# Dilated attention trunk on one core: softmax maxima and sums exchanged by a mask and two short matmuls, merge and turning inside pairs

## The chip, the cores and the metric

One core of a Trainium2 chip, one launch. The time is the device time of that core in microseconds (us). TensorE (PE) multiplies, VectorE (DVE) and ScalarE (ACT) work on elements, GpSimd (POOL) does a little of both and issues adding DMAs, SyncE (SP) issues the other DMAs. Each engine runs its own instructions in order; semaphores tie them together.

## The reference

A trunk of two layers over 512 tokens of width 1024, in float32. Layer 0 mixes tokens by three groups of dilated sliding-window attention, layer 1 by causal pooling; each is followed by a SwiGLU FFN (2816 wide), and a last RMSNorm. The part that matters here is the attention: eight heads of 128, each in three groups.

```python
ATTN_PAIRS = ((128, 1), (512, 4), (2048, 16))     # window, dilation
def dilated_attention_mixer(h, w_qkv, w_out):
    qkv = (h @ w_qkv).reshape(B, S, N_ATTN_GROUPS, 3, HEADS_PER_GROUP, HEAD_DIM)
    for g, (window, dil) in enumerate(ATTN_PAIRS):
        o, lse = dilated_window_attention(qkv[:, :, g, 0], qkv[:, :, g, 1], qkv[:, :, g, 2], window, dil, slopes[g])
        outs.append(o)
        lses.append(lse)
    o = jnp.stack(outs, axis=0)
    wts = jax.nn.softmax(jnp.stack(lses, axis=0), axis=0)
    o = jnp.sum(wts[..., None] * o, axis=0).reshape(B, S, ATTN_WIDTH)
    return o.astype(h.dtype) @ w_out
```

The three groups' outputs of a head are weighted by their softmax denominators. So a token needs one common maximum and one common sum over the scores of all three groups.

## The kernel before

**Products.** All large products are taken in a 32-bit form that TensorE multiplies in one pass (fp32r), with each operand split into a high and a low part: hi·hi, hi·lo and lo·hi. Weights come by SP DMAs into `raw` buffers; ScalarE rounds them to `whi` (L79), VectorE subtracts to `wlo` (L80). A product of queries and keys of one head and group is done by `seven` (L383): seven half-size products in place of eight, each of 4 x 3 matmuls of 128x256 (L374 to L376), 84 in all. Between the seven products stand `behind(0)` to `behind(6)`; there `pump()` prepares the next weights, and pieces of other work can be hung in through `after`. The weights of a `seven` are sums of blocks: one DMA of GpSimd adds on loading (L139), and VectorE adds twice more (L152, L153), on the same in-order queue that evacuates the products (L414 to L424). `raw` has four buffers, so a load waits until a split has freed one.

**Two orders of tokens.** Groups 1 and 2 see tokens by residue class modulo 4: token 4j+r stands in class r. Group 0 sees them in blocks of 128 consecutive tokens. `scores0(h)` (L551) computes group 0's scores in block order (`s0`, partitions are the tokens of a block, four blocks), `scores12(h)` (L587) those of groups 1 and 2 in class order (`s12`, four classes). Each takes its row maximum and an exponential with its row sum, and leaves them in `st`: index 0 for its own order, index 1 for the other order.

**The exchange.** Each order needs the other's maxima and sums, at other partitions. Each writes its own to a small DRAM tile, `dn` (L581) or `df` (L608), and a second DMA reads it back in the other order (L582, L609): four DMAs a head, 4 KB each in elements of four bytes, all on SP's queue, where the weights are loaded too.

**Merge, turn, output.** `merge(h)` (L612) forms the common maximum, the factors and the reciprocal by small operations (L620 to L626), then scales s0 (L628) and s12 (L631) on VectorE. `turn(h)` transposes 7 blocks of s0 (L640) and 8 of s12 (L646) on TensorE and copies the four PSUM results out, two on VectorE and two on ScalarE. `output(h)` (L650) multiplies by the values and adds the groups.

**Order.** `between(h, g)` says which pieces follow the `seven` of head h and group g: of an odd head's group 0 the values' transposes, of group 1 the merge of the head before, of group 2 its turn and this head's scores0; of an even head's group 0 the merge and an output, and so on. Every piece stands after a whole `seven`. Values of groups 1 and 2 come by `values12` (168 matmuls for two heads). A piece's instructions stand in program order on TensorE, ACT and SP, while VectorE's small merge operations are issued after `mark`, the last subtraction of a product.

Of the kernel before, what the change touches and what calls it, by code (L numbers as in the profile page):

```python
# [14 lines left out]
DRAM = bass.MemoryType.DRAM  # L15
# [34 lines left out]
def trunk(ctx: ExitStack, tc: tile.TileContext, xT, norms, w_first, w_qk, w_qkp, w_v0, w_v0p, w_v12, w_out, w_pair, w_down, w_pin, w_pgrp,  # L50
          dist0, dist12, ident_in, invcnt_in, outT):
# [5 lines left out]
    dpool = ctx.enter_context(tc.tile_pool(name="dpool", bufs=2, space=DRAM))  # L57
# [304 lines left out]
    def by_block(t):  # L362

        return t.rearrange("p (b a j) -> p a j b", a=2, b=NT)

    def by_class(t):

        return t.rearrange("p (a j b) -> p a j b", a=2, b=NT)
# [14 lines left out]
    def seven(T, one, two, scratch, after={}, blocks=False):  # L383


        unit, = units.popleft()
        into, out = (by_block, by_class) if blocks else (both, both)

        def again(v):
            return v.unsqueeze(1).to_broadcast([P, 2, *v.shape[1:]])  # L390
# [23 lines left out]
        nc.vector.tensor_add(into(one), out(p26), again(out(first)[:, 0]))  # L414
# [8 lines left out]
        nc.vector.tensor_sub(into(two), out(p45), again(out(sums)[:, 0]))  # L423
        mark.append(nc.vector.tensor_sub(into(one)[:, 1], out(sums)[:, 1], out(p45)[:, 1]))  # L424
        behind(6)
# [19 lines left out]

    def block(t, b, n=1):
        v = t.rearrange("p (i b) -> p b i", b=NT)
        return v[:, b] if n == 1 else v[:, b:b + n]


    with tc.tile_pool(name="opool", bufs=1) as opool:
        early = opool.tile([P, HEADS, S], F32R, tag="o", name="early")
        with tc.tile_pool(name="apool", bufs=1) as apool:
            d0 = apool.tile([P, 3 * P], F32, name="d0")
            d12 = apool.tile([P, 2 * P], F32, name="d12")
# [4 lines left out]
            def scaled_by(t, p, blocks):  # L460
                nc.vector.tensor_mul(*((by_block(t), by_class(p), by_class(rows["row"])) if blocks else
                                       (t, p, rows["row"])))
# [88 lines left out]
            def scores0(h):  # L551
# [3 lines left out]
                nc.gpsimd.tensor_scalar(b0, d0, -SLOPES[h], None, op0=OP.mult)  # L555
# [3 lines left out]
                st = apool.tile([P, 2, 2, 2, NT], F32, name="st", bufs=2)  # L559
                nm = apool.tile([P, 2, NT], F32, name="nm", bufs=2)  # L560
# [18 lines left out]
                dn = dpool.tile([2, S], F32, name="dn")  # L579
                with nc.allow_non_contiguous_dma(reason="a few numbers a token"):  # L580
                    nc.sync.dma_start(dn.rearrange("s (p b) -> p s b", b=NT), st[:, 0, 0])  # L581
                    nc.sync.dma_start(st[:, 1, 1], dn.rearrange("s (r p) -> p s r", r=NT))  # L582
                A[h] = dict(b12=b12, st=st, nm=nm, s0=s0)

            def scores12(h):
# [20 lines left out]
                df = dpool.tile([2, S], F32, name="df")  # L606
                with nc.allow_non_contiguous_dma(reason="a few numbers a token"):
                    nc.sync.dma_start(df.rearrange("s (r p) -> p s r", r=NT), st[:, 0, 1])  # L608
                    nc.sync.dma_start(st[:, 1, 0], df.rearrange("s (p b) -> p s b", b=NT))  # L609
                A[h]["s12"] = s12  # L610

            def merge(h):  # L612

# [4 lines left out]
                co = apool.tile([P, 2, NT], F32, name="co")  # L618
                with tc.issue_after(mark[-1].ins) if mark else nullcontext():
                    nc.vector.tensor_max(mx, st[:, 0, :, 0, :], st[:, 1, :, 0, :])  # L620
# [8 lines left out]
                for r in range(NT):  # L629
                    v = s12[:, r].rearrange("p g k -> p (g k)")  # L630
                    nc.vector.tensor_scalar(v, v, co[:, 1, r:r + 1], None, op0=OP.mult)  # L631

            def turn(h):

                s0, s12 = A[h]["s0"], A[h]["s12"]
                t0 = apool.tile([P, 7 * P], F32, name="t0")
                for lo, n in ((0, 4), (4, 3)):
                    p = ps()
                    for a in range(n):
                        nc.tensor.transpose(blk(p, a), blk(s0, lo + a), ident)  # L640
                    (nc.scalar.copy if lo else nc.vector.tensor_copy)(blk(t0, lo, n), blk(p, 0, n))
# [7 lines left out]
                A[h].update(t0=t0, t12=t12)  # L649

            def output(h):
# [13 lines left out]
                nc.scalar.copy(block(o0, 0, NT), po.rearrange("p (b i) -> p b i", b=NT))  # L665
# [79 lines left out]
            nc.sync.dma_start(d0, dist0)  # L745
            nc.sync.dma_start(d12, dist12)
# [22 lines left out]
            for u in range(NF, len(QK)):  # L769
                evac(0, u, lead[u].p)  # L770
            VT[:] = [scratch("vt") for c in range(2)]
# [8 lines left out]
            for h in range(1, HEADS):  # L780
                for g in range(3):
                    if h == 1 and g < NSOLO:
                        for c in range(2):
                            evac(h, 2 * g + c, product(0))
                    else:
                        qk = [apool.tile([P, S], F32, name=f"qk{g}{c}") for c in range(2)]
                        seven(T, *qk, scratch, blocks=g == 0)
                        for c in range(2):
                            QKV[h, g, c] = qk[c]
                    for f in between(h, g):  # L790
                        f()
# [29 lines left out]
            turn(last)  # L821
# [332 lines left out]
```

## Time and profile before

| what | us |
|---|---|
| median of three runs | 1291.86 |
| lowest and highest run | 1285.66, 1295.61 |
| profiled execution, its own time | 1300.5 |
| its span, first to last instruction | 1298.7 |
| attention layer with sevens, 60 to 485 us of the span | 425.0 |

The page gives for each engine the busy time, its share of the span, and the number of records. The profile's groups put instructions together by line and shape, with the mean of one in ns and the idle time before them. A wait is named by the instruction that waited and the one that released it; SPq is SP's queue of DMA issues. The granted clock of TensorE was 0.99 over the span. Two further groups of the page show how a `seven` stands in it (busy us, mean ns of one, idle before):

```profile
L374 PE MATMUL ps<-h,whi 128*128 128x256 f32 x252 | 74.0, 294 | 0.8 <-DVE sums L418 0.8
L152 DVE TENSOR_TENSOR raw<-raw 128x512 f32<-128x512 f32 x61 | 41.8, 685 | 39.3 <-issue 39.0
```

A matmul's 0.29 us is its passage through the array; several are under way at once.

### The profile page before, as it was taken

The numbers are of one execution on the slowest core, as the hardware profiler recorded it, in microseconds if no ns is written. First come the engines' busy times: TensorE is split into PE (matmuls) and PEld (weight loads), VectorE is DVE, ScalarE is ACT, GpSimd is POOL, SyncE is SP. The second block draws the span as 40 slices with busy tenths as digits, with TensorE's granted clock in tenths as the row PEclk, the third lists the DMA queues.
The fourth block names the chain that finished last, engine by engine and source line by source line (L and its number), as shares of the span: only waits on it lengthen the run. The fifth ranks groups of instructions, "written<-read, shape, count | busy, mean of one in ns | idle before, by whom it ended". The sixth has DMA issues, their size and how long they took to land.

```text
span 1298.7 us, 20811 instructions
## 1 busy us (share of the span) xinstructions
PE 1261.7 (97%) x8274; PEld 1157.6 (89%) x8274; DVE 930.1 (72%) x1398; ACT 542.4 (42%) x831; POOL 125.5 (10%) x113
## 2 busy tenths in 40 slices
PE   9999899998989889999999999999999999999997
PEld 7889899898989878889988999888788998999986
DVE  6986879686778755478934888557968863688643
ACT  6534444343334334344523555343444542455331
POOL 2111111120210010000001110000120100111000
PEclk9999999999999989999999999999999999999998
DMA  8345565655565562244535775333214644676321
GB/s 288 98 98 148 133 157 127 152 134 138 124 161 125 138 187 82 82 106 118 160 108 153 187 185 144 105 134 130 65 49 98 185 126 139 165 183 173 99 69 66
DMA packets 88321, 172.57 MB, mean 133 GB/s; under 512 B 27792, under 2 KB 30240, under 8 KB 88224
## 3 DMA queue, kind: packets, MB, share of 16 engines
q1 hardware_dynamic: 69808, 136.10, 33.0%
q0 software_dynamic: 17264, 34.09, 15.6%
q8 instruction: 65, 1.06, 0.4%
q10 hardware_dynamic: 1152, 1.05, 0.2%
q14 instruction: 32, 0.26, 0.1%
HBM read 169.05 MB, written 2.16 MB: 132 GB/s over the span
## 4 chain that ended last, share of the span: by engine, by line
PE 68%; issue 12%; DVE 10%; DMA 7%; ACT 1%; POOL 1%; SPq 0%; DVEq 0%; POOLq 0%; ACTq 0%
PE ps L256 10%; PE ps L257 10%; PE ps L374 10%; PE ps L259 10%; PE ps L375 10%; PE ps L376 10%; DMA raw<-w_qkp 3%; DVE wlo L80 2%; DMA df<-st 2%; DMA raw<-w_v 1%; PE ps L594 1%; DMA raw<-w_out 1%; ACT whi L79 1%; PE ps L669 1%; POOL rcol L325 1%
## 5 line engine op out<-in xcount | busy, mean ns | idle before, releaser
L79 ACT ACTIVATE whi<-raw 128x1024 fp32r<-128x1024 f32 (+2 forms) x297 | 294.1, 1000 | 472.1 <-PE ps L257 195.5
L80 DVE TENSOR_TENSOR wlo<-raw,whi 128x1024 fp32r<-128x1024 f32 (+2 forms) x297 | 340.3, 1150 | 176.9 <-ACT whi L79 173.7
L256 PE MATMUL ps<-a,whi 128*128 128x512 f32 (+1 forms) x374 | 141.0, 377 | 0.0
L257 PE MATMUL ps<-a,whi 128*128 128x512 f32 (+1 forms) x374 | 140.9, 377 | 0.0
L259 PE MATMUL ps<-a,wlo 128*128 128x512 f32 (+1 forms) x374 | 140.8, 377 | 0.0
L374 PE MATMUL ps<-tt,whi 128*128 128x256 f32 x384 | 108.7, 283 | 0.0
L375 PE MATMUL ps<-tt,whi 128*128 128x256 f32 x384 | 108.7, 283 | 0.0
L376 PE MATMUL ps<-tt,wlo 128*128 128x256 f32 x384 | 108.7, 283 | 0.0
L259 PEld LDWEIGHTS ps<-a,wlo 128*128 128x128 f32 x374 | 70.4, 188 | 12.9
L257 PEld LDWEIGHTS ps<-a,whi 128*128 128x128 f32 x374 | 70.4, 188 | 12.8
L256 PEld LDWEIGHTS ps<-a,whi 128*128 128x128 f32 x374 | 70.4, 188 | 12.8
L139 POOL DMA_DIRECT2D raw<-w_pair x32 | 38.7, 1208 | 445.5 <-DVE wlo L80 158.9
L374 PE MATMUL ps<-h,whi 128*128 128x256 f32 x252 | 74.0, 294 | 0.8 <-DVE sums L418 0.8
L374 PEld LDWEIGHTS ps<-tt,whi 128*128 128x128 f32 x384 | 73.7, 192 | 0.0
L375 PEld LDWEIGHTS ps<-tt,whi 128*128 128x128 f32 x384 | 73.7, 192 | 0.0
L376 PEld LDWEIGHTS ps<-tt,wlo 128*128 128x128 f32 x384 | 73.7, 192 | 0.0
L375 PE MATMUL ps<-h,whi 128*128 128x256 f32 x252 | 72.6, 288 | 0.0
L376 PE MATMUL ps<-h,wlo 128*128 128x256 f32 x252 | 72.6, 288 | 0.0
L376 PE MATMUL ps<-tb,wlo 128*128 128x256 f32 x256 | 72.4, 283 | 0.0
L375 PE MATMUL ps<-tb,whi 128*128 128x256 f32 x256 | 72.4, 283 | 0.0
L374 PE MATMUL ps<-tb,whi 128*128 128x256 f32 x256 | 72.4, 283 | 0.0
L152 DVE TENSOR_TENSOR raw<-raw 128x512 f32<-128x512 f32 x61 | 41.8, 685 | 39.3 <-issue 39.0
(275 smaller groups left out, 3439.3 us busy)
## 6 DMA issues: line engine op xcount, KB each, us to landing
raw<-w_pair SPq DMA_DIRECT2D x76, 512.0 KB, 4.4
raw<-w_qkp SPq DMA_DIRECT2D x36, 512.0 KB, 4.7
raw<-w_pair POOLq DMA_DIRECT2D x32, 512.0 KB, 7.1
raw<-w_down SPq DMA_DIRECT2D x32, 384.0 KB, 3.1
raw<-w_down SPq DMA_DIRECT2D x32, 320.0 KB, 2.8
raw<-w_v SPq DMA_DIRECT2D x18, 512.0 KB, 5.5
raw<-w_qkp POOLq DMA_DIRECT2D x18, 512.0 KB, 7.2
rawhalf<-w_pair SPq DMA_DIRECT2D x32, 256.0 KB, 3.3
```

The costliest lines, as they stand in the source:

```text
L79: nc.scalar.activation(hi, v, AF.Copy)
L80: nc.vector.tensor_tensor(lo, v, hi.bitcast(F32), op=OP.subtract)
L139: nc.gpsimd.dma_start(self.b.t.rearrange("p (a c) -> p a c", a=2), self.src[:, None, 3 * S:].to_broadcast([P, 2, S]), accum_op=OP.add)
L152: nc.vector.tensor_add(a[:, :S], a[:, :S], b[:, :S])
L256: nc.tensor.matmul(self.p[:, cols], w[0][:, s], mh[:, cols], start=self.done == 0, stop=False)
L257: nc.tensor.matmul(self.p[:, cols], w[0][:, s], ml[:, cols], start=False, stop=False)
L259: nc.tensor.matmul(self.p[:, cols], w[1][:, s], mh[:, cols], start=False, stop=self.done == self.n)
L325: nc.gpsimd.tensor_tensor(r, v, nhalf[:, :nt], op=OP.pow)
L374: nc.tensor.matmul(dst, w.t[0][:, c], th, start=k == 0, stop=False)
L375: nc.tensor.matmul(dst, w.t[0][:, c], tl, start=False, stop=False)
L376: nc.tensor.matmul(dst, w.t[1][:, c], th, start=False, stop=k == K2 - 1)
L594: nc.tensor.matmul(blk(p, 2 * a + g - 1), blk(QKV[h, g, 0], r), blk(QKV[h, g, 1], r), start=True, stop=True)
```

## The change

**Exchange.** A block's tokens are now in natural order, (i r) in a block b: partition 4i+r. In class order the token 128b + 4i + r stands at class r, partition 32b + i before. Queries, keys and values of group 0 are written so that block order and class order differ only within groups of four partitions. Then `merge` makes the other order's numbers itself: `far` is `st` spread by a mask `place` (partition modulo 4), two fp32 matmuls of 128x32 with `swap` (ones where two partitions belong to the same four) add within the fours, a second product with the mask and a reduction pick the right one into `st[:, 1]`. The tiles dn and df, their pool and their four DMAs a head are gone. The constants d0, d12 and swap come in one load, `place` in another; b0 is made by two GpSimd operations.

**Engines.** The scaling of s12 and all four copies of the turn are on ScalarE. The addition of `sums` in a block product is two halves.

**Places.** `turn` is split into `turn0` and `turn12`, and merge, turns, scores0 and output are handed to `seven` as `after` pieces. The last head's scores12 and merge move forward in `values12`. `st` and `nm` have one buffer each.

```diff
@@ by_block, by_class
-        return t.rearrange("p (b a j) -> p a j b", a=2, b=NT)
+        return t.rearrange("p (b i r) -> p r i b", b=NT, r=NT)[:, 2 * a.start:2 * a.stop]
@@ seven
-        nc.vector.tensor_add(out(sums), out(p73), again(into(one)[:, 1]))
+        if blocks:
+            for a in (left, right):
+                nc.vector.tensor_add(in_place(sums, a), in_place(p73, a), into(one, right))
+        else:
+            nc.vector.tensor_add(sums, p73, again(one[:, H2:]))
@@ scores0
-                nc.gpsimd.tensor_scalar(b0, d0, -SLOPES[h], None, op0=OP.mult)
+                nc.gpsimd.tensor_scalar(b0[:, :2 * P], d0, -SLOPES[h], None, op0=OP.mult)
+                nc.gpsimd.tensor_scalar(b0[:, 2 * P:], d0[:, P:], -SLOPES[h], None, op0=OP.mult)
...
-                dn = dpool.tile([2, S], F32, name="dn")
-                with nc.allow_non_contiguous_dma(reason="a few numbers a token"):
-                    nc.sync.dma_start(dn.rearrange("s (p b) -> p s b", b=NT), st[:, 0, 0])
-                    nc.sync.dma_start(st[:, 1, 1], dn.rearrange("s (r p) -> p s r", r=NT))
@@ scores12
-                df = dpool.tile([2, S], F32, name="df")
-                with nc.allow_non_contiguous_dma(reason="a few numbers a token"):
-                    nc.sync.dma_start(df.rearrange("s (r p) -> p s r", r=NT), st[:, 0, 1])
-                    nc.sync.dma_start(st[:, 1, 0], df.rearrange("s (p b) -> p s b", b=NT))
@@ merge
+                far = apool.tile([P, 4 * NT, NT], F32, tag="b12", name="far")
                 with tc.issue_after(mark[-1].ins) if mark else nullcontext():
-                    nc.vector.tensor_max(mx, st[:, 0, :, 0, :], st[:, 1, :, 0, :])
+                    nc.vector.tensor_mul(far, st[:, 0].rearrange("p a s b -> p (a s b)").unsqueeze(2).to_broadcast(
+                        [P, 4 * NT, NT]), place[:, None].to_broadcast([P, 4 * NT, NT]))
+                p = ps()
+                for a in range(2):
+                    nc.tensor.matmul(p[:, a * 32:(a + 1) * 32], swap,
+                                     far[:, (1 - a) * 8:(2 - a) * 8].rearrange("p s r -> p (s r)"), start=True, stop=True)
+                nc.vector.tensor_mul(far.rearrange("p (q r) b -> p q r b", r=NT),
+                                     p[:, :64].rearrange("p (q b r) -> p q r b", b=NT, r=NT),
+                                     place[:, None, None].to_broadcast([P, 4, NT, NT]))
+                nc.vector.tensor_reduce(st[:, 1].rearrange("p a s r -> p (a s r)"), far, axis=AX.X, op=OP.add)
+                nc.vector.tensor_max(mx, st[:, 0, :, 0, :], st[:, 1, :, 0, :])
...
-                    nc.vector.tensor_scalar(v, v, co[:, 1, r:r + 1], None, op0=OP.mult)
+                    nc.scalar.activation(v, v, AF.Copy, scale=co[:, 1, r:r + 1])
@@ turn -> turn0, turn12
-                    (nc.scalar.copy if lo else nc.vector.tensor_copy)(blk(t0, lo, n), blk(p, 0, n))
+                    nc.scalar.copy(blk(t0, lo, n), blk(p, 0, n))
...
-                    (nc.scalar.copy if half else nc.vector.tensor_copy)(
-                        t12[:, 2 * half:2 * half + 2].rearrange("p a g k -> p (a g k)"), p)
+                    nc.scalar.copy(t12[:, 2 * half:2 * half + 2].rearrange("p a g k -> p (a g k)"), p)
@@ between
-                if h % 2:
-                    return {0: [later(turn_values, h - 1)] if h > 1 else [], 1: [later(merge, h - 1)],
-                            2: [later(turn, h - 1), later(scores0, h)] + [later(scores12, h)] * (h == HEADS - 1)}[g]
-                return {0: [later(merge, h - 1), later(output, h - 2)], 1: [later(turn, h - 1), later(scores0, h)],
-                        2: [later(output, h - 1)]}[g]
+                if g == 0:
+                    return {1: [later(merge, h - 1)], 3: [later(turn_values, h - 1)] if h > 1 else []} if h % 2 else {
+                        1: [later(output, h - 2)], 2: [later(merge, h - 1)]}
+                if g == 1:
+                    return {0: [later(turn0, h - 1)], 2: [later(turn12, h - 1)], 4: [later(scores0, h)]}
+                return {2: [] if h % 2 else [later(output, h - 1)]}
@@ the last head's values12
-                    QKV[h // 2, 12, 2] = values12({1: [later(halve, 0), later(halve, 1)],
-                                                   2: [later(halve, 2), later(halve, 3)],
-                                                   4: [later(halve, 4), later(halve, 5)], 6: [later(merge, h)]})
+                    QKV[h // 2, 12, 2] = values12({0: [later(scores12, h)], 1: [later(halve, 0), later(halve, 1)],
+                                                   2: [later(merge, h), later(halve, 2), later(halve, 3)],
+                                                   4: [later(halve, 4), later(halve, 5)]})
```

How the instructions stand, first on SP while head 1's scores are finished and head 2's first weights are loaded (line, DMA, destination and source, shape). Before:

```order
L136 DMA raw<-w_qkp 128x1024
L581 DMA dn<-st 128x2x4
L582 DMA st<-dn 128x8x1
L137 DMA raw<-w_qkp 128x1024
L608 DMA df<-st 128x8x1
L609 DMA st<-df 128x2x4
L136 DMA raw<-w_qkp 128x1024
L137 DMA raw<-w_qkp 128x1024
L138 DMA rawhalf<-w_qkp 128x512
```

and after the change:

```order
L134 DMA raw<-w_qkp 128x1024
L135 DMA raw<-w_qkp 128x1024
L134 DMA raw<-w_qkp 128x1024
L135 DMA raw<-w_qkp 128x1024
L136 DMA rawhalf<-w_qkp 128x512
L134 DMA raw<-w_v0p 128x1024
```

No load of weights stands behind a DMA of the scores any more; before, the second one here stood behind two of them and the third behind four.

Then VectorE where head 2's scores are merged, from the last two subtractions of the product ahead of it. Before, in head 3 behind the product of group 1 (qk):

```order
L423 TENSOR_TENSOR qk_1928<-ps,sums 128x512
L424 TENSOR_TENSOR qk_1927<-sums,ps 128x256
L620 TENSOR_TENSOR mx<-st 128x8
L153 TENSOR_TENSOR raw<-raw 128x512
L621 TENSOR_TENSOR ex<-st,mx 128x16
L152 TENSOR_TENSOR raw<-raw 128x512
L623 TENSOR_TENSOR dd<-ex,st 128x16
L80 TENSOR_TENSOR halflo<-rawhalf,halfhi 128x512
L624 TENSOR_TENSOR mx<-dd 128x8
```

and after the change, in head 3's group 0, behind the product of the values of group 0 (vt):

```order
L425 TENSOR_TENSOR vt<-ps,sums 128x4x32x4
L426 TENSOR_TENSOR vt<-sums,ps 128x2x32x4
L150 TENSOR_TENSOR raw<-raw 128x512
L614 TENSOR_TENSOR far<-st,place 128x64
L151 TENSOR_TENSOR raw<-raw 128x512
L621 TENSOR_TENSOR far<-ps,place 128x64
L78 TENSOR_TENSOR halflo<-rawhalf,halfhi 128x512
L624 TENSOR_REDUCE st<-far 128x16
L625 TENSOR_TENSOR mx<-st 128x8
```

The merge begins two products earlier, its first operation stands one raw addition behind the last subtraction, and three operations (L614, L621, L624) stand ahead of the maximum at L625.

Last TensorE, at the turning of head 1 in head 2 (ident is the unit matrix, ps a PSUM buffer). Before, all of it stands between two sevens:

```order
L376 MATMUL ps<-tx,halflo 128x256
L640 MATMUL ps<-ident,s_883 128x128 x7
L646 MATMUL ps<-ident,s_931 128x128 x8
L564 MATMUL ps<-qk_1156,qk_1155 128x256 x2
L569 MATMUL ps<-qk_1156,qk_1155 128x256
L570 MATMUL ps<-qk_1156,qk_1155 128x128
L374 MATMUL ps<-h,whi 128x256
```

After the change the first transposes stand inside a `seven`, behind the first of its products:

```order
L372 MATMUL ps<-h,whi 128x256
L373 MATMUL ps<-h,wlo 128x256
L645 MATMUL ps<-ident,s_820 128x128 x7
L371 MATMUL ps<-h,whi 128x256
L372 MATMUL ps<-h,whi 128x256
```

The 8 of L656 follow 24 matmuls later and scores0's behind 24 more; the two short matmuls (L618) stand 60 matmuls ahead of L645.

More of the change, by code (lines that the diff above doesn't have):

```diff
@@ L14 @@
 PSUM = bass.MemoryType.PSUM
-DRAM = bass.MemoryType.DRAM
 P = 128
@@ L386, in seven @@
         unit, = units.popleft()
-        into, out = (by_block, by_class) if blocks else (both, both)
+        into, left, right = by_block if blocks else in_place, slice(0, 1), slice(1, 2)
         def again(v):
-            return v.unsqueeze(1).to_broadcast([P, 2, *v.shape[1:]])
+            return v.unsqueeze(1).to_broadcast([P, 2, H2])
         p1, p26, p45, p73 = ps(), ps(), ps(), ps()
@@ L413, in seven @@
         mult(p26[:, H2:], w, 0, T, "2")
-        nc.vector.tensor_add(into(one), out(p26), again(out(first)[:, 0]))
+        nc.vector.tensor_add(into(one), p26, again(first[:, :H2]))
         behind(4)
@@ L422, in seven @@
         w.done()
-        nc.vector.tensor_sub(into(two), out(p45), again(out(sums)[:, 0]))
-        mark.append(nc.vector.tensor_sub(into(one)[:, 1], out(sums)[:, 1], out(p45)[:, 1]))
+        nc.vector.tensor_sub(into(two), p45, again(sums[:, :H2]))
+        mark.append(nc.vector.tensor_sub(into(one, right), sums[:, H2:], p45[:, H2:]))
         behind(6)
@@ L664, in output @@
                 o0 = o[h]
-                nc.scalar.copy(block(o0, 0, NT), po.rearrange("p (b i) -> p b i", b=NT))
+                nc.scalar.copy(in_a_row(o0), po.rearrange("p (b i r) -> p b i r", b=NT, r=NT))
                 po = ps()
@@ L784, in trunk @@
                             evac(h, 2 * g + c, product(0))
-                    else:
-                        qk = [apool.tile([P, S], F32, name=f"qk{g}{c}") for c in range(2)]
-                        seven(T, *qk, scratch, blocks=g == 0)
+                        for fs in between(h, g).values():
+                            for f in fs:
+                                f()
+                    else:
                         for c in range(2):
-                            QKV[h, g, c] = qk[c]
-                    for f in between(h, g):
-                        f()
+                            QKV[h, g, c] = apool.tile([P, S], F32, name=f"qk{g}{c}")
+                        seven(T, QKV[h, g, 0], QKV[h, g, 1], scratch, between(h, g), g == 0)
                 if h == 1:
@@ L820, in trunk @@
             halve(last - 1)
-            turn(last)
+            turn0(last)
+            turn12(last)
             lead.append(Product(HEADS, heads).add(range(last - 1)))
@@ L1138 @@
         "w_pgrp": pg,
[L1139 to L1141 removed]
+        "consts": np.concatenate([past, near, np.where(d4 >= 0, 4.0 * d4, FAR),
+                                  np.where((d4 >= 0) & (d4 % 4 == 0), 4.0 * d4, FAR),
+                                  i[:, None] // NT == i[None, :] // NT,
+                                  i[:, None] % NT == np.arange(NT)[None, :]], 1).astype(np.float32),
         "ident_in": np.eye(P, dtype=np.float32),
```

44 lines of the change are left out of this document (20 added, 24 removed).

## The prediction

> **What bounds the kernel now.** I read the page's busy times first, then the waits of TensorE, then the granted clock by windows, and last, for each wait, the timeline back to what released it.
>
> ```profile
> PE 1261.7 (97%) x8274; PEld 1157.6 (89%) x8274; DVE 930.1 (72%) x1398; ACT 542.4 (42%) x831; POOL 125.5 (10%) x113
> ```
>
> TensorE is busy in 97% of the 1298.7 us. So only its idle time and its slow-clock time can be won, and what it is given in addition is paid in full. Its waits (line, what it waited for, us in all, times, longest):
>
> ```profile
> PE ps L640 <- DVE s L628: 12.4, 6, 3.3
> PE ps L256 <- ACT oh L79: 5.7, 1, 5.7
> PE ps L569 <- DVE qk L414: 5.1, 4, 1.5
> ...
> PE ps L594 <- DVE qk L423: 0.9, 1, 0.9
> ```
>
> The first four, 12.4 + 5.7 + 5.1 + 0.9 = 24.1 us, lie in the attention layer, where the change is: the turning of a head's scores (L640) waits for their scaling on VectorE. The clock adds to it. The next rows are windows: length, then busy time and records of PE, PEld, DVE, ACT, POOL, then granted clock, DMA share, GB/s.
>
> ```profile
> 102.00:112.00 10.00, 10.00 (x85) 10.00 (x85) 7.65 (x9) 3.31 (x5) 0.69 (x2) 1.00 0.66 107
> 257.92:261.33 3.41, 1.68 (x10) 1.44 (x11) 3.41 (x5) 0.00 (x0) 0.00 (x0) 1.00 1.04 239
> 261.33:264.74 3.41, 3.41 (x18) 3.41 (x18) 3.41 (x7) 0.37 (x1) 0.00 (x0) 0.50 0.55 179
> 322.77:326.18 3.41, 3.41 (x15) 3.05 (x14) 3.41 (x7) 1.07 (x2) 0.80 (x1) 0.50 0.36 132
> 380.79:384.21 3.42, 3.42 (x18) 3.42 (x18) 3.42 (x7) 0.37 (x1) 0.00 (x0) 0.50 0.49 165
> 442.23:445.65 3.42, 3.42 (x13) 2.86 (x12) 3.42 (x6) 0.80 (x2) 0.00 (x0) 0.50 0.36 127
> 476.37:483.19 6.82, 5.54 (x18) 4.62 (x19) 5.42 (x16) 2.48 (x5) 0.00 (x0) 0.50 0.81 287
> 60.00:485.00 425.00, 400.12 (x3088) 386.10 (x3087) 323.37 (x516) 175.24 (x314) 57.12 (x56) 0.98 0.57 140
> ```
>
> At full clock a product's matmul takes 10.00/85 = 0.12 us. Four windows of 3.41 us and one of 6.82 ran at half clock: 20.5 us that did the work of 10.2. Each follows a wait: in 257.92 to 261.33 TensorE did 1.68 us of work and idled 1.73, and the next window has clock 0.50. So a wait of this size costs about 1.7 us more than itself. VectorE fills those windows entirely (3.41 of 3.41): it is behind.
>
> Why it is behind, at head 1's end (start, length, engine, line, operation):
>
> ```profile
> 101.80 0.47 SPq L137 DMA_DIRECT2D raw<-w_qkp  x1
> 102.33 0.44 SPq L608 DMA_DIRECT2D df<-st  x1
> 116.48 0.36 SPq L609 DMA_DIRECT2D st<-df  x1
> 116.96 0.71 SPq L136 DMA_DIRECT2D raw<-w_qkp  x1
> ```
> ```profile
> 106.06 2.36 DVE L80 TENSOR_TENSOR wlo<-raw,whi 128x1024 fp32r<-128x1024 f32 x2 [0.16 <-ACT whi L79]
> ...
> 132.49 0.69 DVE L152 TENSOR_TENSOR raw<-raw 128x512 f32<-128x512 f32 x1 [4.36 <-issue]
> ...
> 136.64 0.16 DVE L620 TENSOR_TENSOR mx<-st 128x8 f32<-128x8 f32 x1
> ...
> 139.30 1.11 DVE L628 TENSOR_SCALAR s<-s,co 128x256 f32<-128x256 f32 x4
> ```
> ```profile
> 139.80 1.04 PE L640 MATMUL ps<-ident,s 128*128 128x128 f32 x7 [2.07 <-DVE s L628]
> ```
> ```profile
> SPq L609 <- DMA df<-st: 92.0, 8, 13.7
> ...
> SPq L582 <- DMA dn<-st: 25.7, 7, 5.4
> ```
>
> SP's queue issues nothing from 102.33 to 116.48, since L609 waits for the small transfer that L608 wrote. Behind it stands the weight load of 116.96, whose buffer was free at 108.4 (106.06 + 2.36): 8.5 us late. That load's sums are needed at L152, where VectorE then stands for 4.36 us; so the merge begins at 136.64, the scaling at 139.30, and the transposes wait 2.07. SP loses 92.0 + 25.7 us so over the heads.
>
> **What the change costs and gives.**
>
> *The four DMAs a head are removed.* The 117.7 us of SP waits go. Late by 8.5 us becomes late by about nothing, which covers the 4.36 at L152 and the 2.07 behind it. The 5.7 us at L256 have the same cause:
>
> ```profile
> 465.92 0.36 SPq L609 DMA_DIRECT2D st<-df  x1
> 466.37 3.98 SPq L115 DMA_DIRECT2D raw<-w_out  x3
> ```
> ```profile
> 455.42 0.49 ACT L605 ACTIVATE s<-s,nm 128x256 f32<-128x256 f32 x1
> ...
> 469.76 1.06 ACT L79 ACTIVATE whi<-raw 128x1024 fp32r<-128x1024 f32 x1 [6.20 <-DMA raw<-w_out]
> 476.02 1.06 ACT L79 ACTIVATE whi<-raw 128x1024 fp32r<-128x1024 f32 x1 [5.20 <-DMA raw<-w_out]
> ```
>
> Three loads of w_out start right behind L609, ScalarE stands 6.20 and 5.20 us for them, and the 5.69 on TensorE follow. I take 24.1 off, and the 10.2 of half clock with it, since every half-clock window hangs on one of these waits: 34.3.
>
> *The exchange on TensorE.* Eight heads by 2 matmuls of 128x32 in plain fp32. The trace has none of this shape; short fp32 ones from both sides of its width:
>
> ```profile
> 27.90 0.80 PE ps L320 x8
> ...
> 95.18 1.79 PE ps L594 x16
> ```
>
> These are rows of the chain of waits: 0.80/8 = 0.100 us of 128x1, 1.79/16 = 0.112 of 128x128. L594's 8 instructions of a head (4 classes, 2 groups) are 16 records, so an fp32 matmul is two passes, and 16 instructions are 32: 3.2 to 3.6 us, nothing hidden since they stand between products; I take 3.5. [...]
>
> *The exchange on VectorE.* Two products of 128x64, a reduction to 128x16 (bounds 0.16 from L620's 128x8 and 0.62 from a 128x256; I take 0.2 each, near the small one): 0.6 a head. The sum of a block product in two halves adds about 0.2. Against that the s12 scaling and two copies leave it. ScalarE takes them up:
>
> ```profile
> L631 DVE TENSOR_SCALAR s<-s,co 128x256 f32<-128x256 f32 x32 | 9.2, 348 | 0.0
> L641 DVE COPY t<-ps 128x512 f32<-128x512 f32 x8 | 5.4, 678 | 0.0
> L605 ACT ACTIVATE s<-s,nm 128x256 f32<-128x256 f32 x32 | 15.8, 497 | 2.5 <-DVE nm L602 2.5
> ```
>
> VectorE: 9.2/8 + 2 x 0.68 = 2.5 off, 0.8 on, so 1.7 us a head easier. ScalarE: 4 x 0.50 and 2 x about 0.6 = 3.2 a head, 26 in all; it had 175 of 425 us in this stage, so 47%. Cost on TensorE nothing, if the scaling is in time: the s12 transposes now stand 84 matmuls and 7 transposes behind the short ones, 10.1 + 0.6 = 10.7 us; the chain to them is far exchange 0.4, merge 2.66 (136.64 to 139.30), four scalings 2.0, some 5.5 with a semaphore's hop each. 5.2 us are in hand.
>
> *Merge and turning go inside products.* The transposes at L640 now stand 60 matmuls (7.2 us) behind the short matmuls, with 0.4 + 2.66 + 1.11 = 4.2 needed. What is late next is the short matmul itself, which waits for far, i.e. for the last subtraction of the product before. At an odd head:
>
> ```profile
> 170.94 0.28 PE L374 MATMUL ps<-h,whi 128*128 128x256 f32 x1
> ```
> ```profile
> 173.97 0.64 DVE L424 TENSOR_TENSOR vt<-sums,ps 128x256 f32<-128x256 f32 x1
> 174.43 0.69 DVE L153 TENSOR_TENSOR raw<-raw 128x512 f32<-128x512 f32 x1
> ```
>
> It is due some 27 matmuls (two products of 12, and the depth of the pipeline) behind 170.94, at 174.2; far follows L424 and one raw addition, at 174.4 + 0.6 + 0.2 = 175.2. One us, at heads 3, 5 and 7: 3.0. At the even heads it stands behind one more product (12 matmuls, 1.4) and an output, and has some 3 us in hand. At the last head, scores12 would end near 449, the short matmul 48 matmuls later near 454.7, and far needs the exponential that ends at 455.91 (455.42 + 0.49): 1.5 with far's own time. One of these four waits may trip the clock once more: 1.7. New waits together 6.2.
>
> *Constants in one load, b0 by two POOL instructions, one buffer of st and nm, another copy pattern for o0:* nothing on TensorE; POOL is busy 10%, and scores0 rewrites st some 110 rows of TensorE (13 us) behind the short matmuls, when the merge's 2.66 are long over. On SP two DMAs of d become one, with one small more, all behind the first weights.
>
> Sum: 34.3 - 3.5 - 6.2 = 24.6 off. The profiled execution took 1300.5 us (span 1298.7), 8.6 above the median 1291.86 of the runs; it would come to 1275.9, and the median to 1267.
>
> **The rivals.**
>
> *R1, the weights stay late.* In the chain of waits one load took 11.40 where the median of its kind is 4.7:
>
> ```profile
> 101.80 11.40 DMA raw<-w_qkp
> ```
> ```profile
> raw<-w_qkp SPq DMA_DIRECT2D x36, 512.0 KB, 4.7
> ```
>
> If loads issued earlier only crowd each other, L152's wait of 4.4 stays at the three even heads, and there L640's 12.4/6 = 2.1, L569's 5.1/4 = 1.3 and 1.7 of half clock: 5.1 each, 15.3 less won, 9.3 off, 1283. Against it: the DMA share is 0.57 in the stage.
>
> *R2, slower: ScalarE's order.* The s12 scalings stand in ScalarE's order behind weight splits, and a split waits for its load:
>
> ```profile
> ACT whi L79 <- DMA raw<-w_qkp: 47.2, 7, 8.9
> ```
>
> A split that stands 8.9 us before the scaling exceeds the 5.2 in hand by 3.7; with 1.7 of half clock 5.4 at each of seven heads is 38: 1267 + 38 = 1305. From 24.6/7 = 3.5 us a head it is slower than before. Against it: the loads come earlier once SP is free.
>
> *R3, the exchange was hidden and VectorE is simply full.* It is busy 323 of 425 us, and 3.41 of 3.41 where TensorE waits. Then only the w_out gap goes, 5.7 and its 3.4 of half clock, less 3.5: 5.6 off, 1286. Against it: VectorE stood 4.36 us idle at 132.49, just before.
>
> [...]
>
> **How the numbers follow.** Chances: forecast 0.72, R1 0.13, R3 0.09, R2 0.06. The forecast's own range is 1257 (all 34.3 won and nothing new) to 1277 (twice the new waits and two more half-clock windows, 6.2 + 3.4 worse). For 8 in 10 it reaches to R1: 1256 to 1284. A measurement of this kernel can tell about 1% from no change, 12.9 us: faster is under 1278.9, slower over 1304.8. Faster: the forecast and a quarter of R1, 0.75; same: the rest of R1, R3 and half of R2, 0.22; slower: 0.03.
>
> **What would show it.** SP's waits for dn and df gone, and no weight load later than 1 us behind its buffer; VectorE's 4.36 at L152 under 1; TensorE's waits for s0's scaling under 1 us in all, those for far some 4.5; the half-clock windows 0 to 2 instead of six; 32 short passes at 0.10 to 0.11. I am wrong if L152 still stands 4 us (R1), if the s12 transposes wait for ScalarE (R2), or if VectorE stays full over 3.41 us windows with TensorE idle (R3).

## The result, and the profile after

| | us |
|---|---|
| before, median of four runs | 1292.38 (1285.66 to 1295.61) |
| changed kernel, median of four runs | 1271.95 (1271.64 to 1273.39) |
| ratio, 95% interval | 0.9851 (0.9811 to 0.9891) |
| profiled execution of the changed kernel: its time, its span | 1271.68, 1269.9 |

Faster by 1.5%: 20.4 us in medians, 28.8 us between the two profiled executions. The runs of before spread over 10 us, those of the changed kernel over 2. The two differences and the two spreads return below.

TensorE's waits in the changed kernel (line, what it waited for, us in all, times, longest):

```profile
PE ps L618 <- DVE far L614: 3.2, 4, 0.9
PE ps L645 <- ACT s L636: 1.6, 1, 1.6
PE ps L331 <- POOL rcol L323: 1.3, 2, 1.1
```

Of the 24.1 us of waits in the attention layer nothing is left. Two new ones are there: the short matmuls (L618) wait four times for far, and head 0's first transposes (L645) once. Next the three stages of the front half, as windows of before and then of the changed kernel: up to the first `seven` of head 2, from there to the last product of the heads, and the projection w_out (length, busy time and records of PE, PEld, DVE, ACT, POOL, granted clock, DMA share, GB/s).

```profile
0.00:114.10 114.10, 112.63 (x604) 97.50 (x605) 91.54 (x144) 56.66 (x102) 16.46 (x18) 1.00 0.52 152
114.10:469.00 354.90, 335.71 (x2708) 328.65 (x2707) 272.64 (x426) 148.04 (x263) 48.07 (x44) 0.98 0.57 139
469.00:529.90 60.90, 55.21 (x270) 46.58 (x270) 33.32 (x54) 23.55 (x34) 2.67 (x5) 0.94 0.42 145
```
```profile
0.00:117.40 117.40, 114.25 (x607) 98.35 (x608) 92.38 (x144) 61.05 (x110) 16.68 (x20) 1.00 0.52 157
117.40:448.90 331.50, 328.33 (x2737) 326.67 (x2736) 268.81 (x430) 171.07 (x306) 49.53 (x51) 1.00 0.60 150
448.90:501.00 52.10, 52.10 (x269) 44.52 (x269) 28.42 (x38) 21.42 (x32) 2.60 (x5) 1.00 0.40 134
```

The sevens take 23.4 us less, the projection 8.8, the first stage 3.3 more, of which 1.6 is the wait at L645 and 0.4 head 0's short matmuls. The clock is 1.00 in all three: no half-clock window is left. SP at the same place, head 1's end:

```profile
105.14 0.33 SPq L135 DMA_DIRECT2D raw<-w_qkp  x1
110.65 0.33 SPq L134 DMA_DIRECT2D raw<-w_qkp  x1
111.79 0.33 SPq L135 DMA_DIRECT2D raw<-w_qkp  x1
```

The load that was issued at 116.96 is issued at 110.65, though the stage began 3 us later. It waits for its buffer (VectorE's split of the load before runs from 109.40 to 110.62), not for a small DMA.

### The profile page after: what moved, and what is told of

Its sections match the earlier page's. It is cut to its first block, busy times and chain, and to the rows that moved or that the text cites. A ratio compares the mean times of both kernels' runs of the same rounds, so it can differ in the third digit from the quotient of the medians.

```text
span 1269.9 us, 20876 instructions
## 1 busy us (share of the span) xinstructions
PE 1252.9 (99%) x8306; PEld 1154.4 (91%) x8306; DVE 922.3 (73%) x1383; ACT 567.6 (45%) x879; POOL 127.2 (10%) x121
## 4 chain that ended last, share of the span: by engine, by line
PE 79%; issue 11%; DVE 7%; ACT 2%; POOL 1%; DMA 0%; DVEq 0%; POOLq 0%; ACTq 0%
PE ps L371 12%; PE ps L372 12%; PE ps L373 12%; PE ps L255 10%; PE ps L254 10%; PE ps L257 10%; PE ps L483 2%; PE ps L485 2%; PE ps L484 2%; DVE wlo L78 1%; PE ps L678 1%; PE ps L590 1%; ACT whi L77 1%; POOL rcol L323 1%; DVE n L302 1%
## 5 line engine op out<-in xcount | busy, mean ns | idle before, releaser
L255 PEld LDWEIGHTS ps<-a,whi 128*128 128x128 f32 x374 | 70.4, 188 | 12.7
L371 PE MATMUL ps<-h,whi 128*128 128x256 f32 x252 | 72.5, 288 | 0.0
L372 PE MATMUL ps<-h,whi 128*128 128x256 f32 x252 | 71.3, 283 | 0.0
L254 PE MATMUL ps<-h,whi 128*128 128x512 f32 x160 | 62.7, 392 | 0.0
```

The source lines that it names most:

```text
L254: nc.tensor.matmul(self.p[:, cols], w[0][:, s], mh[:, cols], start=self.done == 0, stop=False)
L255: nc.tensor.matmul(self.p[:, cols], w[0][:, s], ml[:, cols], start=False, stop=False)
L371: nc.tensor.matmul(dst, w.t[0][:, c], th, start=k == 0, stop=False)
L372: nc.tensor.matmul(dst, w.t[0][:, c], tl, start=False, stop=False)
```

## The experiments

Each kernel's time stands beside runs of before on the same chip; the ratio has its 95% interval.

**1. The read-backs later on SP, first attempt (e1_late_read).** On the kernel before:

```diff
 def merge(h):
+    nc.sync.dma_start(st[:, 1, 1], dn ...)     # moved from scores0
+    nc.sync.dma_start(st[:, 1, 0], df ...)     # moved from scores12
```

> The kernel before, with one thing changed: the two DMAs that read the exchanged numbers back are issued at the head of merge, one product later, so that SP's queue no longer stands in front of the weights; the exchange still goes through memory, and no short matmul exists. Theory (the gain is SP's queue set free): SP's waits for dn and df fall from 118 us to under 20, VectorE's 4.4 us before L152 fall under 1, the 5.7 us before the output projection and most half-clock windows go, time 1266 to 1276. Rival (VectorE is simply full, or the exchange itself is what costs): the turn still waits 10 us and more, time 1285 to 1293.

1288.48 us, ratio 0.9943 (0.9914 to 0.9971). It did not test what it meant to: the two read-backs stand in SP's order where they stood, right behind their writes: st<-dn at 103.06 and st<-df at 117.93, in front of the next weight load at 118.41. Moving the call in the program didn't move the DMA in the queue. The section on the kernel before says that a piece's instructions stand in program order on SP; for these DMAs they don't. SP's waits tell the same:

```profile
SPq L615 <- DMA df<-st: 89.6, 8, 15.2
SPq L614 <- DMA dn<-st: 27.8, 7, 5.8
```

117 us, as before. The time is in the rival's range, but with SP's waits unchanged it decides nothing between the two. The 5.7 us ahead of the projection went, and two windows ran at half clock instead of six.

**2. The changed kernel with the exchange by DMA (e2_places_dma).**

```diff
-    far, two matmuls with swap, far, reduce                    # in merge
+    nc.sync.dma_start(dn.rearrange("s (b p) -> p s b", b=NT), st[:, 0, 0])      # in scores0
+    nc.sync.dma_start(st[:, 1, 1], dn.rearrange("s (p r) -> p s r", r=NT))
+    nc.sync.dma_start(df.rearrange("s (p r) -> p s r", r=NT), st[:, 0, 1])      # in scores12
+    nc.sync.dma_start(st[:, 1, 0], df.rearrange("s (b p) -> p s b", b=NT))
```

> The changed kernel with its places and engines, but the exchange again by four DMAs a head on SP, where they stood before. Theory (the DMAs on SP are the cost, and the earlier merge now also meets them): SP waits for df and dn some 100 us again, weights late, VectorE's merge two products earlier stands for the read-back up to 6 us, TensorE's waits 25 us and more, time 1290 to 1320. Rival (the new places and engines make the gain): 1268 to 1278.

1271.88 us, ratio 0.9824 (0.9789 to 0.9858): the time of the changed kernel, and a miss of the theory as it was put. SP waits 66.9 us for dn and 36.1 for df, 103.0 in all, as expected; but TensorE waits only 6.8 us for the turn, where 25 and more were expected. So it isn't the sum of SP's waits that sets the time. In this kernel the numbers read back belong to other tokens; their amount is right. The reason is that the section on the change has the two orders the wrong way round: the token 128b + 4i + r has partition 4i + b in class order in both kernels, and it is block order that went from 32r + i to 4i + r. The expectation had also overlooked that the token order changes how the DMAs cut the tile. Here df is written in runs of four floats, and dn in single ones. Issues of this kernel (KB each, median us to landing):

```profile
dn<-st SPq DMA_DIRECT2D x8, 4.0 KB, 10.8
st<-dn SPq DMA_DIRECT2D x8, 4.0 KB, 4.4
df<-st SPq DMA_DIRECT2D x8, 4.0 KB, 5.9
```

Before, df was the one of single floats:

```profile
dn<-st SPq DMA_DIRECT2D x8, 4.0 KB, 3.8
df<-st SPq DMA_DIRECT2D x8, 4.0 KB, 12.6
```

So this run left a question: is it the places or df's 12.6 us?

**3. The exchange by matmul alone (e3_exchange_only).** The changed kernel with `between`, the last head's places, the engines, and the two buffers of st and nm of before:

```diff
-    return {1: [later(merge, h - 1)], ...                 # places inside a seven
+    return {0: [later(merge, h - 1), later(output, h - 2)], ...    # behind whole sevens
```

> The changed kernel's exchange by mask and short matmuls alone, at the places and on the engines of before (merge behind a whole product, turn in one piece, scaling and half the copies on VectorE). Theory: SP's waits are gone, but the short matmuls now stand right behind the product whose last subtraction their far waits for: 1.5 to 2.5 us at 7 heads and some half-clock windows, time 1277 to 1292. Rival (the places cost and give nothing): 1269 to 1274.

1303.98 us, ratio 1.0061 (1.0039 to 1.0083): slower than before, and beyond the range. Its waits:

```profile
PE ps L618 <- DVE far L614: 21.9, 7, 3.5
...
PE ps L645 <- DVE s L633: 0.6, 1, 0.6
```

The turn's 12.4 us are gone, as SP's queue would have it. But the short matmul stands right behind the product whose last subtraction it waits for, 2.3 to 3.5 us at seven heads, and the clock pays on top: eight windows of 3.41 us at half clock, of which this row shows the first two:

```profile
128.84:135.67 6.83, 5.91 (x27) 5.91 (x28) 3.33 (x12) 1.09 (x2) 2.23 (x3) 0.50 0.55 147
```

**4. The engines back (e4_engines).** The changed kernel with `nc.vector.tensor_scalar` for s12 and two of four copies on VectorE.

> The changed kernel with the s12 scaling and half of the turn's copies back on VectorE. Theory (VectorE has room once the weights are early): TensorE's waits grow by under 3 us in all, time 1272 to 1276. Rival (VectorE was full, ScalarE's help makes the gain): TensorE waits for s0's or s12's scaling by 2 us a head with half-clock windows, 1282 to 1292.

1272.74 us, ratio 0.9819 (0.9793 to 0.9845), within 1 us of the changed kernel. ScalarE's help is worth nothing that can be measured; VectorE had room.

**5. The places alone (e5_places_only).** The kernel before with the new `between`, `turn0`, `turn12` and the last head's places; exchange, layout and engines as before.

> The kernel before with the new places alone: merge, turn0, turn12, scores0 and output inside the products, the last head's scores12 and merge moved forward; the exchange through memory with its layout, SP's queue, and the engines as before. Theory (the places carry the gain, the exchange through memory would do): SP still waits 100 us and more for dn and df, but TensorE's waits are under 10 us, time 1266 to 1276. Rival (places and exchange are needed together: the merge two products earlier stands for a read-back that takes 12.6 + 2.2 us): VectorE waits for st 5 us and more at each odd head, TensorE's waits over 15 us with half-clock windows, time 1282 to 1300.

1311.9 us, ratio 1.0126 (1.009 to 1.0163): slower, as the rival said and by more. VectorE in head 3, then TensorE:

```profile
174.06 0.69 DVE L152 TENSOR_TENSOR raw<-raw 128x512 f32<-128x512 f32 x1
181.82 0.17 DVE L620 TENSOR_TENSOR mx<-st 128x8 f32<-128x8 f32 x1 [7.07 <-DMA st<-df]
```
```profile
188.41 1.73 PE L640 MATMUL ps<-ident,s 128*128 128x128 f32 x7 [4.99 <-DVE s L628]
```

Two products earlier the maximum comes ahead of its numbers; VectorE stands 7.07 us in its own queue, 37.6 in five such waits, and everything behind it is late. So each half of the change alone makes the kernel slower (1304, 1312 against 1292 to 1296); the two together make it faster. And the places of this kernel with a df in runs of four floats, which is experiment 2, took 1271.88 us: 40 less. (The engines differ too, which by experiment 4 makes no difference that can be measured, and so do dn and the small changes to sums, constants and buffers.)

**6. The new waits taken away (e6_later, after_again).** The changed kernel with merge one place later at odd heads (1 to 2) and at the last (2 to 3), and head 0's turn behind the first product of head 1's group 2; and the changed kernel once more beside it.

> The changed kernel with the new waits taken away: merge one product later at odd heads (behind the third instead of the second) and at the last head, and head 0's turn half a group later in head 1. Theory (each of the five waits is only the distance between the last subtraction and the short matmul, or between the scaling and its transposes): the four far waits of 0.9 and the one of 1.6 at L645 are gone, 5.4 us less than the changed kernel, 1265 to 1268. Rival (the wait moves on to the turn or to scores0): within 2 us of the changed kernel, 1270 to 1274.

> The changed kernel once more beside the others: 1271 to 1274, no half-clock window in the attention layer, the same five waits.

1270.24 us (1268.51 to 1270.6), ratio 0.9802 (0.9761 to 0.9844), against 1271.8 (1271.23 to 1272.35), ratio 0.9819 (0.9785 to 0.9853). The waits at L645 and at the last head went, the three at odd heads stayed (2.3 us in all): far moved along with the matmuls, two operations down VectorE's order. So the theory's 1265 to 1268 was missed: the time lies in the rival's range, though not for the rival's reason, since the waits that stayed are those for far and none moved on to the turn.

**7. Only what follows far moved (e10_far_first).** far's first product becomes a piece of its own (`spread_out`) at the old place, the rest of merge one place later:

```diff
-    return {1: [later(merge, h - 1)], 3: ...
+    return {1: [later(spread_out, h - 1)], 2: [later(merge, h - 1)], 3: ...
```

> The changed kernel with far's first product kept where it is and only what follows moved one product later, at odd heads and the last; head 0's turn half a group later as in the run before. Theory (the short matmul stands too near behind far): the three waits of 0.8 that stayed when far moved along are gone, TensorE waits under 0.5 us in the attention layer, time 1266.5 to 1269. Rival (the wait moves on to the turn): 1269.5 to 1272.

1266.35 us (1264.76 to 1266.57), ratio 0.9777 (0.9748 to 0.9806). No wait for far is left, and the time is 5.6 under the changed kernel's 1271.95, in two sets of runs.

**8. The kernel before, once more (before_look1).**

> The kernel before once more, for its profile. Theory (a wait halves the next clock window only if it falls into one window of a fixed grid, so the count changes from execution to execution): the half-clock total in the attention layer is not 20.5 us again but anywhere from 3 to 25, and the time moves by half of it against the recorded profile. Rival (the half clock is a fixed part of these waits): 20.5 us again, with the same five places.

1294.88 us, a single run. Only two windows of the attention layer are at half clock, against six: 6.8 us against 20.5. They are the first two rows; the third is the stage of the sevens.

```profile
440.94:444.35 3.41, 3.20 (x15) 3.21 (x16) 3.41 (x7) 0.24 (x1) 0.00 (x0) 0.50 0.38 137
471.67:475.08 3.41, 3.41 (x8) 2.49 (x9) 3.41 (x7) 1.19 (x3) 0.00 (x0) 0.50 0.82 315
115.00:464.50 349.50, 332.15 (x2709) 324.52 (x2708) 272.37 (x426) 149.05 (x264) 47.91 (x45) 1.00 0.59 142
```

The sevens took 349.5 us instead of 354.9, so the half clock is not a fixed part of these places in the kernel. The time moved by 5.6 us against 6.8 of lost clock and 3.4 of shorter waits (20.7 against 24.1); the rest of the program varied the other way by some 2, and what is left I can't place.

**9. df in runs of 16 bytes (e8_df_runs).** The kernel before with one pattern changed:

```diff
-    nc.sync.dma_start(df.rearrange("s (r p) -> p s r", r=NT), st[:, 0, 1])
+    nc.sync.dma_start(df.rearrange("s (p r) -> p s r", r=NT), st[:, 0, 1])
```

> The kernel before, with df written in runs of 16 bytes in place of single elements of 4; DMA count, queue, places and engines as before. (The numbers that come back belong to other tokens: the exchange is misplaced, its amount is the same.) Theory (SP's queue behind df's 12.6 us is what makes the weights late): df lands in 4 to 6 us, SP's wait for it falls from 92 to 30 to 45 us, VectorE's wait at L152 from 39 to under 20, TensorE's waits from 24 to under 12, time 1274 to 1283. Rival (the old places cost, whatever the queue does): 1287 to 1295.

1263.7 us, ratio 0.9758 (0.9724 to 0.9792): ten under the range of the theory and more than the whole change gives, with the old places, engines and DMAs. The write and what it does on SP:

```profile
df<-st SPq DMA_DIRECT2D x8, 4.0 KB, 4.3
```
```profile
103.29 0.41 SPq L608 DMA_DIRECT2D df<-st  x1
110.15 0.36 SPq L609 DMA_DIRECT2D st<-df  x1
110.63 0.39 SPq L136 DMA_DIRECT2D raw<-w_qkp  x1
```
```profile
124.13 0.69 DVE L152 TENSOR_TENSOR raw<-raw 128x512 f32<-128x512 f32 x1
124.74 1.06 DVE L418 TENSOR_TENSOR sums<-ps,qk 128x512 f32<-128x512 f32 x1
125.71 1.22 DVE L80 TENSOR_TENSOR wlo<-raw,whi 128x1024 fp32r<-128x1024 f32 x1
```
```profile
PE ps L594 <- DVE qk L423: 1.5, 1, 1.5
```

The load comes at 110.63 instead of 116.96, L152 stands where it needn't wait (124.13; before 132.49 behind 4.36 us of idling), and TensorE's attention waits are 1.5 us in place of 24.1. This is the prediction's chain link by link, with one DMA's run length as the only edit. SP still waits 60.1 us for the two small writes (32.0 for df, 28.1 for dn) of 117.7; what was left costs TensorE almost nothing.

**10. The read-backs later, tied to loads (e9_late_read2).** As 1, with `tc.issue_after` on the last weight load.

> The kernel before with the read-backs really behind weight loads on SP: they are tied behind the last load that is issued before merge, five or six loads behind the writes (in the first attempt the order on SP had stayed as it was). Exchange through memory, places and engines as before. Theory (SP's queue): SP's waits for dn and df under 20 us, VectorE at L152 under 20 us, TensorE's waits under 10, time 1268 to 1278. Rival (places): 1287 to 1295. A third way: the read-back now comes late for merge, and VectorE waits for st; then the waits at the turn stay though L152's are gone.

1278.29 us, the median of 1276.95, 1278.29 and 1281.84 (a fourth run of 2273.61, at a granted clock of 0.79, is like no other and is left aside), ratio 0.9878 (0.9839 to 0.9916). SP now waits 24.1 us for dn and df instead of 117.7, VectorE 29.0 at L152 instead of 39.0, TensorE 12.0 in the attention layer instead of 24.1. The way of the theory, but each sign misses its range, and the gain is about half of experiment 9's: some read-backs still meet a write that has not landed (10.9 us the longest), and stand in front of the loads behind them.

**11. df in runs of 16 bytes, at the right tokens (e11_df_runs_right).** The kernel before; df is laid out so that a pattern of three dimensions can read it:

```diff
-    df = dpool.tile([2, S], F32, name="df")
+    df = dpool.tile([NI, 2, NT, NT], F32, name="df")
-    nc.sync.dma_start(df.rearrange("s (r p) -> p s r", r=NT), st[:, 0, 1])
-    nc.sync.dma_start(st[:, 1, 0], df.rearrange("s (p b) -> p s b", b=NT))
+    for s in range(2):
+        nc.sync.dma_start(df[:, s], st[:, 0, 1, s])
+    for r in range(NT):
+        nc.sync.dma_start(st[r * NI:(r + 1) * NI, 1, 0].rearrange("p s b -> p (s b)"),
+                          df[:, :, :, r].rearrange("i s b -> i (s b)"))
```

> The kernel before with df written in runs of 16 bytes and read back at the right tokens: two writes (maxima, sums) and four reads of 32 partitions a head in place of one and one; places, engines, token order and the exchange through memory as before. Theory (the four-byte writes of df in front of the weights were the whole cost): SP's waits for df 30 to 50 us, VectorE's wait at L152 15 to 20, TensorE's waits in the attention layer under 5, time 1263 to 1270, so at or below the changed kernel. Rival (four-byte reads and four more DMAs a head cost SP what the write saved): df's waits over 70 us, 1278 to 1292.

1267.62 us (1265.91 to 1269.41), ratio 0.9791 (0.9758 to 0.9823). Its waits and writes:

```profile
PE ps L594 <- DVE qk L423: 1.8, 1, 1.8
PE ps L256 <- ACT oh L79: 1.5, 1, 1.5
```
```profile
df<-st SPq DMA_DIRECT2D x16, 2.0 KB, 4.0
```

VectorE's wait at L152, 26.8 us, is over the 15 to 20 that were expected; SP's for df, 34.6, and TensorE's in the attention layer, 3.9, are in their ranges. With four more DMAs a head it is still 4.3 us under the changed kernel's 1271.95 (in other runs, but the two ranges do not touch). A few lines of layout give what the change gives; with the new waits taken away (7) the matmuls reach the same, 1266.35, and I can't tell these two apart.

## Why the prediction was right, point by point

**The chain from SP to the turn: right, and shown.** Experiment 9 changes one write pattern and the whole chain goes with it, 24.1 us of waits to 1.5. Experiment 11 does the same with the numbers at the right tokens. Rival R3 (VectorE simply full) falls with it: VectorE has the same work there (272.7 us busy in the stage of the sevens, 272.6 before). R1 (weights stay late) didn't come: the loads land in 4.2 us in the median, and ScalarE's waits for w_qkp are gone from its list. VectorE stood 39.0 us at L152, 27.3 of them at seven places of the attention layer; in the changed kernel that addition (L150) waits 12.3 us at four places, and all four lie behind 550 us, after the attention layer. R2 didn't come either; in experiment 4 it makes no difference who scales s12. The sum in two halves, the constants' loads and the single buffers were not run alone.

What the prediction did not see is how little of the change that needs. It took SP's wait behind df for a price of going through memory; it is the price of single floats: with the pattern alone changed, 12.6 us became 4.3 (experiment 9). The row for dn, 3.8 us for the same 4 KB against df's 12.6, stood in the profile of before. All writes of dn and df of 4 KB in these runs agree, by their medians: 10.8 to 12.7 us in single floats, 3.7 to 5.9 in runs of four.

**The clock: 10.2 us taken off, right for this execution.** All half-clock windows of the attention layer hung on waits and are gone with them. **One new window, 1.7 us: wrong.** Waits of 0.8 to 1.6 us tripped nothing: the clock is 1.00 in all three stages.

**The short matmuls, 3.5 us: 3.0 measured.** At a head without a wait (start, length, records):

```profile
124.95 0.28 PE L373 MATMUL ps<-tx,wlo 128*128 128x256 f32 x1
125.07 0.53 PE L618 MATMUL ps<-far,const 128*128 128x32 f32 x4
125.44 0.36 PE L371 MATMUL ps<-t,whi 128*128 128x256 f32 x1
```

Four passes from 125.07 to the next product's start at 125.44: 0.37 a head, 0.09 a pass. This is near the 0.100 of the narrow rows.

**VectorE's exchange, 0.6 a head: 0.65.** The three are 0.22, 0.22 and 0.21 us.

**The far waits, 3.0 and 1.5: 2.3 and 0.9.** At the four places that were named. Left out was a fifth: head 0's turn in head 1, whose products are not sevens, so that turn0 follows its merge too closely; 1.6 us at L645. Experiment 7 took all five away.

**From the sum to the median: the step that failed.** "It would come to 1275.9, and the median to 1267." The profiled execution came to 1271.68 and the median to 1271.95. The sum worked out from one execution was set off in full against the median of others. But the 8.6 us by which the profiled execution lay above the median were not a constant on top: waits and half-clock windows vary from execution to execution (in one execution of before 24.1 us of waits and 20.5 at half clock, in the other 20.7 and 6.8, experiment 8), and the change removes just those. What varies and goes must be taken from the execution it was read in; the time after is then one number for both. So the 1275.9 was the forecast to keep. It is 4.2 too high: 1.7 for the window that didn't trip, 0.5 for the passes, some 1.3 for the waits at far, less the 1.6 at L645, and about 1.1 for the transposes, which the list of waits doesn't show; 3.0 in all, and 1.2 stay open. The transposes' groups before and after (busy us, mean ns):

```profile
L646 PE MATMUL ps<-ident,s 128*128 128x128 f32 x64 | 10.3, 307 | 0.0
L640 PE MATMUL ps<-ident,s 128*128 128x128 f32 x56 | 8.7, 288 | 12.4 <-DVE s L628 12.4
```
```profile
L656 PE MATMUL ps<-ident,s 128*128 128x128 f32 x64 | 8.3, 273 | 0.0
L645 PE MATMUL ps<-ident,s 128*128 128x128 f32 x56 | 7.7, 274 | 1.6 <-ACT s L636 1.6
```

19.0 us became 16.0. Before, 3.7 us of them lay in half-clock windows (0.56 of L640 and 3.17 of L646), so 1.9 of the 3.0 are in the 10.2 already; that leaves the 1.1. That these come from transposes released one by one as the scalings ended is argued, not shown.

So the mechanism was right and is shown. That the median came within 5 us of 1267 is in part luck: the base that was 8.6 off and the sum that was 4.2 short lie on opposite sides. 24.6 us were forecast, 28.8 were won between the profiled executions and 20.4 between the medians.

## What to carry to other kernels

Before a small exchange is moved off memory, look at how long its DMAs take against each other: of two with the same bytes, the slow one may only need longer runs (12.6 us in single floats, 4.3 in runs of four). What it costs shows in the waits of TensorE, not in the sum of the queue's waits: 103 us of these on SP went with 6.8 on TensorE in experiment 2, 117.7 with 24.1 before. A gain that is read from one profiled execution is set against that execution's own time; where the runs of before spread and the change removes what makes them spread, the median before is no base. A piece that waits for the end of a product belongs one place behind the piece that feeds it (experiment 7: no wait for far is left, 5.6 us less). And a change of two halves can gain where each half alone loses (1272 us together, 1304 and 1312 alone), so a half is not to be judged alone.

## What the runs showed of the hardware that was not expected

In these profiles the granted clock fell by windows of 3.41 us on a fixed grid: the half-clock windows of before start at 261.33, 322.77, 380.79, 442.23 and 476.37 us, which are 18, 17, 18 and 10 windows apart. Whether one came went with TensorE's idle time inside the window ahead of it (its length less TensorE's busy time). Of the full-clock windows of before, those with 1.73, 1.82, 1.87, 1.97, 2.62 and 3.41 us of idle were followed by a half-clock window; none of those with 1.55 or less was. In the changed kernel one with 1.87 (from 1259.52, at the very end) was, and one with 1.61 (from 78.51) was not. Where between 1.61 and 1.73 it turns, or whether one figure holds for every execution, these two profiles do not show. In experiment 3 TensorE idled 3.24 us up to 129.76, and half clock came from 128.84 to 135.67. It idled another 3.24 between 245.76 and 252.59 (2.58 up to 249.17, 0.66 behind it); the grid's boundary 35 windows behind 128.84, at 248.3, splits that into some 1.7 and 1.5 if it was one piece (an estimate), and the clock stayed at 1.00.

So two waits of one length cost differently, it seems by where they fell: the first was followed by 6.83 us at half clock, some 3.4 of lost work (an estimate, half of 6.83), the second by none. One execution of before had 20.5 us at half clock, another 6.8, and its waits were 3.4 us shorter. Of the eleven runs of before beside experiments 1 to 4, the fastest (1289.10 us) had a mean granted clock of 0.995 and the slowest (1299.86 us) one of 0.988, which is some 9 us of lost clock out of the 10.8 between them; one run, with 0.941 at 1298.68 us, doesn't fit.
